# DeltaNet inverse: block transposes on VectorE and a second merge on 64x64 blocks

## Chip, cores, metric

One core of one Trainium2 chip runs the whole kernel. The metric is device microseconds from launch to end; the kernel before was timed in three runs. Engines: TensorE (PE; PEld are its weight loads), VectorE (DVE), ScalarE (ACT), GpSimd (POOL), SyncE (SP, which here issues DMAs).

## The reference

A trunk of two layers over 1024 tokens of 1024 features, all in float32. The first layer mixes tokens with a gated DeltaNet (8 heads of 128), the second with latent attention; a SwiGLU follows each, and adaLN modulates each. Only the DeltaNet is touched. Per head and chunk of tokens it computes

```python
L = where(strict, einsum(kb, k) * decay, 0)     # strictly lower triangular
u = triangular_solve(L + I, v * beta)           # the kernel forms (I + L)^-1 itself
w = triangular_solve(L + I, kb * exp(g_cum))
attn = einsum(q, k) * decay
# then chunk by chunk, with a carried state S:
#   y = u - w S;  o = q_dec S + attn y;  S = S * exp(g_last) + k_dec^T y
```

and after it a norm, a gate and an output projection. The kernel uses chunks of 128 tokens, so each head has 8 matrices L of 128x128.

## The kernel before

The DeltaNet works head by head. For head h the steps are: K (project keys and queries, `gdn_proj`: 24 products of 128x512 for each half of the tokens at line 202, then a convolution on DVE at line 334), A (`gdn_prep_a`: L of each chunk), V (values and gate), B (`gdn_prep_b`: the transposed inverse U and the masked attention `at`), R (`gdn_rec`: the recurrence over 8 chunks). They are written in the order B of head h+1, R of head h, then K, A, V of head h+2. A planner with a cost model then sets the order of instructions on each engine: it takes what is ready by its model, in order of priority, so projections of a later head fill PE between the small products of B and R. On the chip each engine then runs its own list in that fixed order, and semaphores hold an instruction until its operands are there.

`gdn_prep_b` inverts I + L in two stages. First the four 32x32 diagonal blocks of all 8 matrices at once on DVE: ACT copies them out (line 412), a DVE transpose spreads them over partitions (414), 31 steps of two DVE instructions solve (421, 423), and another DVE transpose brings them back as Xn (425). Then, for four matrices at a time ("half"), two merges:

- A zeroed tile Xs (memset on POOL, 438) gets the inverse diagonal blocks by four ACT copies (441). Xs is block diagonal.
- Merge s = 32: PE transposes Xs (446), ACT copies the result into U (448). U is to hold the transposed inverse. PE multiplies L by the odd blocks of U (459, into `pw`), ACT copies it (461, `w`), PE multiplies by Xs (464, `pv`), and DVE writes the negated blocks into U (466).
- Merge s = 64: the same with 64x64 blocks: PE transposes the whole of U (446), ACT copies it into a second Xs (451), PE multiplies L by the right half of U (459), ACT copies w (461), PE multiplies by Xs (464), DVE writes one 64x64 block (466). All these products contract over 128 partitions and have weights of 128 columns, although only one 64x64 block of the result is used.

In float32 each product is two PE instructions, each with its own weight load; a transpose is one. The SBUF pool `gw` has one buffer for each name unless stated, so both Xs share one slot and each `w` waits for the one before it to be read. The PSUM pool `pe` has two banks, named "e". Tiles called junk take the elementwise output of instructions of which only the row sums are used (lines 379, 400, 520).

Of the kernel before, what the change touches and what calls it, by code (L numbers as in the profile page):

```python
# [9 lines left out]
F32 = mybir.dt.float32  # L10
# [9 lines left out]
P = 128  # L20
# [12 lines left out]
class Trunk:  # L33
# [10 lines left out]
    # ---------------------------------------------------------------- constants  # L44
# [64 lines left out]
    # ---------------------------------------------------------------- adaLN  # L109
    def ada_steps(self, l, m, pool, acc):  # L110
        """acc += the rows of ada_w, each times its c; a step to a row tile"""
# [17 lines left out]
    def ada_ahead(self, l, ms, ps, acc, tag):  # L129
        """the parts ms of layer l, a row tile at a time"""  # L130
        for m in ms:
            yield from self.ada_steps(l, m, self.wraw, acc)
            (self.ada_row if m in (2, 5) else self.ada_cols)(l, m, ps, None, tag, acc)
            yield
            yield
            yield
# [12 lines left out]
    def ada_row(self, l, m, ps, pool, tag="ada_p", acc=None):  # L149
        """mod part m of layer l as a row in DRAM"""  # L150
# [23 lines left out]
    # ---------------------------------------------------------------- weights  # L174
# [5 lines left out]
    def load_w(self, src, shape=(KT, P), bufs=None, pool=None, mul=None, tag="w"):  # L180
        """a weight block of up to [P, 1024] as its two float32r parts"""
# [13 lines left out]
    def mm3(self, out, lts, rts):  # L195
        """sum over pairs of ((lhsT hi, lo), (rhs hi, lo)) of their product, less lo*lo"""
        nc = self.nc
        seq = []
        for (lh, ll), (rh, rl) in zip(lts, rts):
            seq += [(lh, rh), (lh, rl), (ll, rh)]  # L200
        for i, (l, r) in enumerate(seq):
            nc.tensor.matmul(out, l, r, start=(i == 0), stop=(i == len(seq) - 1))  # L202

    # ---------------------------------------------------------------- norm
    def rstd_of(self, x, pool, n=D, junk=None):
        """(mean(x^2)+eps)^-0.5 over the row of x [P, n]"""
# [10 lines left out]
    def rpow(self, out, in_):  # L217
        """in_ ** -0.5"""
        self.nc.gpsimd.tensor_tensor(out=out, in0=in_, in1=self.mh[:, 0:in_.shape[1]], op=ALU.pow)  # L219

    # ---------------------------------------------------------------- gated DeltaNet
    def gdn_gates(self, hi, lo, pool, ps):
        """per-token scalars, token-major, column h*8+chunk: beta, g in parts, exp of the sums of g"""
# [77 lines left out]
    def gdn_proj(self, h, names, hi, lo, res, first=None):  # L301
        """conv and silu of q, k, v and silu of z for head h, feature-major"""
        nc = self.nc
        for nm in names:
# [6 lines left out]
            for s in range(2):  # L311
                # the first two by halves of the features: the first half is there before the other
# [23 lines left out]
                # the taps are halved: silu(2 u) = u (1 + tanh u)  # L336
# [7 lines left out]
    def gdn_decay(self, h, qd, flip, tag):  # L344
        """exp of the sum of g over (j, i], for tokens i >= j of 4 chunks; row i, or row j if flip"""
# [17 lines left out]
    def gdn_prep_a(self, h, kq):  # L363
        """L of each chunk, row i by column j, and the per-token scalars that go with it"""
# [6 lines left out]
        for qd in range(2):  # L371
# [5 lines left out]
            for i in range(4):  # L377
                junk = self.gw.tile([P, P], BF16, name="junk", bufs=2)
# [19 lines left out]
            for i in range(4):  # L398
                junk = self.gw.tile([P, P], BF16, name="junk2", bufs=2)
# [3 lines left out]
    def gdn_prep_b(self, h, kq, pr):  # L403
        """at: the masked attention by source token; U: the transpose of (I + L)^-1"""
# [3 lines left out]
        # 32x32 diagonal blocks, one matrix (and one of 4 column groups) to a partition  # L408
# [26 lines left out]
        for m0 in range(0, M, 4):  # L435
            mh = slice(m0, m0 + 4)
            Xs = self.gw.tile([P, 4, P], F32, name="Xs")
            nc.gpsimd.memset(Xs, 0.0)
# [4 lines left out]
            for s in (32, 64):  # L443
                px = self.pe.tile([P, 4, P], F32, name="e")
                for i in range(4):
                    nc.tensor.transpose(px[:, i], Xs[:, i] if s == 32 else U[:, m0 + i], self.ident)
                if s == 32:
                    nc.scalar.copy(U[:, mh], px)
                else:
                    Xs = self.gw.tile([P, 4, P], F32, name="Xs")  # L450
                    nc.scalar.copy(Xs, px)
                pw = self.pe.tile([P, 4, 64], F32, name="e")
                for i in range(4):
                    m = m0 + i
                    if s == 32:
                        rhs = U[:, m].rearrange("p (a b c) -> p a b c", b=2, c=32)[:, :, 1]
                    else:
                        rhs = U[:, m, 64:128]
                    nc.tensor.matmul(pw[:, i], L[:, m], rhs, start=True, stop=True)  # L459
                w = self.gw.tile([P, 4, 64], F32, name="w")  # L460
                nc.scalar.copy(w, pw)
                pv = self.pe.tile([P, 4, 64], F32, name="e")
                for i in range(4):
                    nc.tensor.matmul(pv[:, i], Xs[:, i], w[:, i], start=True, stop=True)  # L464
                for b in range(0, 4, 2) if s == 32 else (0,):
                    v.tensor_scalar(out=U[b * 32:b * 32 + s, mh, b * 32 + s:b * 32 + 2 * s],
                                    in0=pv[b * 32:b * 32 + s, :, b * 16:b * 16 + s], scalar1=-1.0, op0=ALU.mult,
                                    scalar2=None)
        pr.update(at=at, U=U)

    def gdn_rec(self, h, kq, pr):
# [4 lines left out]
        for half in range(2):  # L476
            on = self.gw.tile([P, 4, P], F32, name="on")
            ss = self.gs.tile([P, 4], F32, name="ss")
            for cc in range(4):
# [39 lines left out]
                junk = self.gw.tile([P, P], BF16, name="junk3", bufs=2)  # L519
                nc.scalar.activation(out=junk, in_=on[:, cc], func=AF.Square, accum_out=ss[:, cc:cc + 1])  # L520
            # rms norm of o with the scale of q folded in
# [17 lines left out]
    def gdn_prologue(self, hi, lo):  # L539
        """the first norm: x goes feature-major while the modulation is worked out, one half of the features first"""  # L540
# [6 lines left out]
        with ExitStack() as st:  # L547
# [10 lines left out]
            def ada(half):  # L558
                """the parts 0 and 1 of the modulation, for half of the features"""
# [52 lines left out]
            # x0[(b, r, m), i, c] = (i == 8 r + c)  # L612
# [9 lines left out]
    def gdn(self, right, outer):  # L622
# [5 lines left out]
        with ExitStack() as s2:  # L628
# [21 lines left out]
            self.gs = s2.enter_context(tc.tile_pool(name="gs", bufs=2))  # L650
            kqv, pr = [{} for _ in range(H)], {}
# [46 lines left out]
    # ---------------------------------------------------------------- output projection  # L698
    def out_w(self, heads, w_out, gate, own=None):
        """rows of w_out for these heads, times the gate"""  # L700
# [3 lines left out]
    def out_row(self, t, h0, ws, x_src, x, raw, oh, ol, bank):  # L704
        """x = a row of x_src + gate * (o @ w_out) over the heads from h0 on"""
# [11 lines left out]
    def out_rows(self, h0, ws, x_src, op, bank, done, raw_t):  # L717
        """row tile by row tile; done(t, row) takes each"""
# [7 lines left out]
    def out_pools(self, l, right):  # L726
        """for the weights of two heads and for rows; they stay open in right"""
# [3 lines left out]
    def gdn_out(self, w_out, x_src, right, bank, before):  # L731
        """the first four heads, to x_dram; the weights of the others stay"""
# [14 lines left out]
    # ---------------------------------------------------------------- SwiGLU  # L747
    # gate and up (rows 1 and 2) of one block of ff, times the halves of d, times the halves of the tokens:
    # one step of Strassen's product in Winograd's form,
    #   S1 = A21 + A22, S2 = S1 - A11, S3 = A11 - A21, S4 = A12 - S2  # L750
    #   T1 = B12 - B11, T2 = B22 - T1, T3 = B22 - B12, T4 = T2 - B21
    #   P1 = A11 B11, P2 = A12 B21, P3 = S4 B22, P4 = A22 T4, P5 = S1 T1, P6 = S2 T2, P7 = S3 T3
    #   U2 = P1 + P6, U3 = U2 + P7
    #   C11 = P1 + P2, C12 = U2 + P5 + P3, C21 = U3 - P4, C22 = U3 + P5
# [9 lines left out]
    def ffn_pair(self, t, xs, pool, ps):  # L764
        """token tiles 2 t and 2 t + 1 (rows xs) into the right-hand operands; B1, B2 are the even and the odd tiles"""
# [736 lines left out]
```

## Time and profile before

| | us |
|---|---|
| median of 3 runs | 2642.77 (2641.49 to 2646.53) |
| span of the profiled execution, first to last instruction | 2633.9 |
| PE busy | 2519.0 (96%) |
| DVE busy | 1957.7 (74%) |
| ACT busy | 1182.6 (45%) |
| POOL busy | 182.6 (7%) |

The profiled execution's time from launch to end is not given apart from its span. The page says for each engine how long it was busy, and follows a chain back from the last instruction through whatever released each step. A busy share over the whole span mixes stages: the DeltaNet runs from about 100 to 740 us, and stretches and waits of it are asked for separately. An instruction's duration on PE includes its way through the array, so products that follow each other closely have starts nearer together than their durations.

### The profile page before, as it was taken

Reading aid. Unit: us, or ns where it says so; the run is one execution under the profiler, and the core shown is the slowest. Engines: PE = TensorE matmul, PEld = TensorE weight load, DVE = VectorE, ACT = ScalarE, POOL = GpSimd, SP = SyncE. Lnnn points to the kernel's source line nnn. Section 1 sums busy time; section 2 is a strip of 40 time slices with the busy share of each in tenths; the row PEclk is TensorE's granted clock in tenths of the full one; section 3 lists DMA queues with packets and bytes.
Section 4 is the critical chain, followed back from the end, with each engine's and each line's share of the span. In section 5 each row is a group of like instructions: output and inputs, shape, how many; then the busy total and the mean of one; then the engine's idle time right before and its main releaser. Section 6 shows DMA issues by size and latency. Waiting matters only on the chain.

```text
span 2633.9 us, 35735 instructions
## 1 busy us (share of the span) xinstructions
PE 2519.0 (96%) x12821; PEld 2074.6 (79%) x12821; DVE 1957.7 (74%) x3732; ACT 1182.6 (45%) x2390; POOL 182.6 (7%) x337
## 2 busy tenths in 40 slices
PE   5999899999899999999999899999999999999998
PEld 4777777777778888888888798888779888887786
DVE  5886788888758887877586766667568777774778
ACT  5555455555556222323334575555374233232433
POOL 1211112221000000000000010000010000000000
PEclk8999999999999999999999999999999999999999
DMA  6111222321544544545854521112653332335634
GB/s 227 41 33 33 73 73 85 93 89 49 168 160 158 168 151 152 176 130 176 281 173 147 160 74 59 47 51 77 202 175 97 105 104 92 108 104 211 237 96 144
DMA packets 258705, 327.62 MB, mean 124 GB/s; under 512 B 17578, under 2 KB 176448, under 8 KB 258528
## 3 DMA queue, kind: packets, MB, share of 16 engines
q1 hardware_dynamic: 235840, 284.37, 34.4%
q10 hardware_dynamic: 22688, 40.97, 4.1%
q8 instruction: 101, 1.65, 0.3%
q14 instruction: 76, 0.62, 0.1%
HBM read 247.16 MB, written 78.14 MB: 124 GB/s over the span
## 4 chain that ended last, share of the span: by engine, by line
PE 77%; DVE 11%; ACT 4%; DMA 3%; POOL 2%; issue 2%; SPq 0%; POOLq 0%; DVEq 0%; ACTq 0%
PE pd L965 14%; PE nrm_p L202 14%; PE pj L202 13%; PE pd L202 10%; PE P L202 7%; PE pd L1282 3%; PE po L202 2%; DVE cacc L334 2%; PE pq L202 1%; PE tp L1325 1%; PE e L464 1%; PE e L459 1%; DVE X L423 1%; ACT Xs L441 1%; DVE st L421 1%
## 5 line engine op out<-in xcount | busy, mean ns | idle before, releaser
L965 PE MATMUL pd<-wlo,gh 128*128 128x512 f32 x616 | 243.4, 396 | 2.3 <-DVE wlo L178 1.9
L965 PE MATMUL pd<-whi,gl 128*128 128x512 f32 x616 | 241.4, 394 | 1.3 <-DVE gl L178 1.2
L965 PE MATMUL pd<-whi,gh 128*128 128x512 f32 x616 | 236.7, 394 | 5.0 <-ACT gh L177 4.6
L202 PE MATMUL pj<-hThi,whi 128*128 128x512 f32 x480 | 196.5, 409 | 0.0
L202 PE MATMUL pj<-hThi,wlo 128*128 128x512 f32 x480 | 196.0, 408 | 0.0
L202 PE MATMUL pj<-hTlo,whi 128*128 128x512 f32 x480 | 194.8, 406 | 0.0
L177 ACT CAST gh<-wraw 128x1024 fp32r<-128x1024 f32 x84 | 82.3, 979 | 247.5 <-PE pd L965 208.8
L177 ACT CAST whi<-wraw 128x1024 fp32r<-128x1024 f32 (+3 forms) x105 | 100.6, 960 | 136.8 <-DMA wraw<-in_ffn_w_gate_dram 50.2
L219 POOL TENSOR_TENSOR nrm_r<-nrm_r,mh 128x1 f32<-128x1 f32 x56 | 37.7, 674 | 1594.1 <-DVE nrm_r L213 1585.1
L965 PEld LDWEIGHTS pd<-wlo,gh 128*128 128x128 f32 x616 | 116.2, 189 | 33.5 <-DVE wlo L178 8.3
L178 DVE TENSOR_TENSOR gl<-wraw,gh 128x1024 fp32r<-128x1024 f32 x84 | 95.3, 1134 | 62.2 <-ACT gh L177 62.0
L965 PEld LDWEIGHTS pd<-whi,gh 128*128 128x128 f32 x616 | 116.0, 188 | 32.1 <-ACT gh L177 5.9
L178 DVE TENSOR_TENSOR wlo<-wraw,whi 128x1024 fp32r<-128x1024 f32 (+3 forms) x105 | 117.2, 1116 | 28.2 <-ACT whi L177 26.9
L965 PEld LDWEIGHTS pd<-whi,gl 128*128 128x128 f32 x616 | 116.2, 189 | 27.4 <-DVE gl L178 2.2
L202 PE MATMUL nrm_p<-T,xrow 128*128 128x512 f32 (+1 forms) x576 | 133.7, 386 | 0.0
L202 PE MATMUL nrm_p<-T,ow_hi 128*128 128x512 f32 (+1 forms) x600 | 132.0, 368 | 0.0
L202 PE MATMUL nrm_p<-T,ow_lo 128*128 128x512 f32 (+1 forms) x552 | 125.8, 376 | 0.0
L202 PEld LDWEIGHTS nrm_p<-T,xrow 128*128 128x128 f32 x576 | 105.1, 188 | 23.7
L202 PEld LDWEIGHTS nrm_p<-T,ow_hi 128*128 128x128 f32 x600 | 103.6, 188 | 20.8 <-ACT fh L785 0.2
L202 PEld LDWEIGHTS nrm_p<-T,ow_lo 128*128 128x128 f32 x552 | 97.8, 188 | 20.6
L334 DVE SCALAR_TENSOR_TENSOR cacc<-cr,cwc,cacc 128x512 f32<-128x512 f32 x144 | 108.7, 761 | 6.0 <-ACT cacc L332 5.5
L202 PEld LDWEIGHTS pj<-hThi,wlo 128*128 128x128 f32 x480 | 91.5, 191 | 15.4
(527 smaller groups left out, 6459.9 us busy)
## 6 DMA issues: line engine op xcount, KB each, us to landing
wraw<-in_ada_w_dram SPq DMA_DIRECT2D x80, 512.0 KB, 4.2
wraw<-in_ffn_w_gate_dram SPq DMA_DIRECT2D x44, 512.0 KB, 4.1
wraw<-in_ffn_w_up_dram SPq DMA_DIRECT2D x44, 512.0 KB, 4.6
gd_S<-sx ACTq DMA_DIRECT2D x88, 256.0 KB, 2.6
B<-in_ffn_w_down_dram SPq DMA_DIRECT2D x40, 512.0 KB, 6.6
wraw<-gd_S SPq DMA_DIRECT2D x40, 512.0 KB, 4.5
gd_A<-co ACTq DMA_DIRECT2D x66, 256.0 KB, 2.7
wraw<-in_gdn_w_in_dram SPq DMA_DIRECT2D x32, 512.0 KB, 4.1
```

Source lines behind the costliest of these rows:

```text
L177: nc.scalar.copy(hi, raw)
L178: nc.vector.tensor_tensor(out=lo, in0=raw, in1=hi.bitcast(F32), op=ALU.subtract)
L202: nc.tensor.matmul(out, l, r, start=(i == 0), stop=(i == len(seq) - 1))
L219: self.nc.gpsimd.tensor_tensor(out=out, in0=in_, in1=self.mh[:, 0:in_.shape[1]], op=ALU.pow)
L334: nc.vector.scalar_tensor_tensor(out=acc, in0=cr[:, j:j + 512], scalar=self.cw[:, j, ch:ch + 1], in1=acc, op0=ALU.mult, op1=ALU.add)
L421: v.tensor_tensor(out=t[:, 0:n], in0=Lr[:, j, j + 1:32].rearrange("p (i o) -> p i o", o=1).broadcast_to([P, n, 8]), in1=X[:, j:j + 1].broa ...
L423: v.tensor_tensor(out=X[:, j + 1:32], in0=X[:, j + 1:32], in1=t[:, 0:n], op=ALU.subtract)
L441: nc.scalar.copy(Xs[pb, :, b * 32:b * 32 + 32].rearrange("p m (r c) -> p m r c", c=8), Xn[pb, :, :, mh].rearrange("p c r m -> p m r c"))
L459: nc.tensor.matmul(pw[:, i], L[:, m], rhs, start=True, stop=True)
L464: nc.tensor.matmul(pv[:, i], Xs[:, i], w[:, i], start=True, stop=True)
L965: nc.tensor.matmul(acc[t], x[:, j, ts], y[:, j], start=(j0 + j == 0 and k == 0), stop=(j0 + j == NJ - 1 and k == 2))
L1282: nc.tensor.matmul(sc[:, 0:nm], q[:, ts], k[:, cs], start=(i == 0), stop=(i == 4 and not last))
```

## The change

In `gdn_prep_b` Xs becomes one tile for all heads, zeroed once before the loop; the ACT copies overwrite its diagonal blocks each time. A DVE transpose of 32x32 blocks writes U from Xs directly, in place of four PE transposes and the ACT copy. The first merge is otherwise as before. The second merge takes the lower left 64x64 block of L (partitions 64 to 127) as weights and the lower right block of U; it transposes only the upper left 64x64 block of U on PE, and both copies and the last product are 64 partitions wide. Three junk tiles go from two buffers to one, two of them under one name. Comments are taken out.

```diff
@@ gdn_prep_a and gdn_rec
-                junk = self.gw.tile([P, P], BF16, name="junk", bufs=2)
+                junk = self.gw.tile([P, P], BF16, name="junk")
-                junk = self.gw.tile([P, P], BF16, name="junk2", bufs=2)
+                junk = self.gw.tile([P, P], BF16, name="junk2")
-                junk = self.gw.tile([P, P], BF16, name="junk3", bufs=2)
+                junk = self.gw.tile([P, P], BF16, name="junk2")
@@ gdn_prep_b
-            Xs = self.gw.tile([P, 4, P], F32, name="Xs")
-            nc.gpsimd.memset(Xs, 0.0)
+            Xs = self.xs
...
-            for s in (32, 64):
-                px = self.pe.tile([P, 4, P], F32, name="e")
-                for i in range(4):
-                    nc.tensor.transpose(px[:, i], Xs[:, i] if s == 32 else U[:, m0 + i], self.ident)
-                if s == 32:
-                    nc.scalar.copy(U[:, mh], px)
-                else:
-                    Xs = self.gw.tile([P, 4, P], F32, name="Xs")
-                    nc.scalar.copy(Xs, px)
...
+            v.transpose(out=U[:, mh], in_=Xs)
+            pw = self.pe.tile([P, 4, 64], F32, name="e")
+            for i in range(4):
+                rhs = U[:, m0 + i].rearrange("p (a b c) -> p a b c", b=2, c=32)[:, :, 1]
+                nc.tensor.matmul(pw[:, i], L[:, m0 + i], rhs, start=True, stop=True)
+            w = self.gw.tile([P, 4, 64], F32, name="w")
+            nc.scalar.copy(w, pw)
+            pv = self.pe.tile([P, 4, 64], F32, name="e")
+            for i in range(4):
+                nc.tensor.matmul(pv[:, i], Xs[:, i], w[:, i], start=True, stop=True)
+            for b in (0, 2):
+                pb = slice(b * 32, b * 32 + 32)
+                v.tensor_scalar(out=U[pb, mh, b * 32 + 32:b * 32 + 64], in0=pv[pb, :, b * 16:b * 16 + 32],
+                                scalar1=-1.0, op0=ALU.mult, scalar2=None)
+
+            lo, up = slice(0, 64), slice(64, 128)
+            px = self.pe.tile([64, 4, 64], F32, name="e")
+            pw = self.pe.tile([64, 4, 64], F32, name="e")
+            for i in range(4):
+                nc.tensor.matmul(pw[:, i], L[up, m0 + i, lo], U[up, m0 + i, up], start=True, stop=True)
+            for i in range(4):
+                nc.tensor.transpose(px[:, i], U[lo, m0 + i, lo], self.ident[lo, lo])
+            w = self.gw.tile([P, 4, 64], F32, name="w")
+            nc.scalar.copy(w[lo], pw)
+            x = self.gw.tile([64, 4, 64], F32, name="xw")
+            nc.scalar.copy(x, px)
+            pv = self.pe.tile([64, 4, 64], F32, name="e")
+            for i in range(4):
+                nc.tensor.matmul(pv[:, i], x[:, i], w[lo, i], start=True, stop=True)
+            v.tensor_scalar(out=U[lo, mh, up], in0=pv, scalar1=-1.0, op0=ALU.mult, scalar2=None)
@@ gdn, before the loop over heads
+            self.xs = self.gw.tile([P, 4, P], F32, name="Xs")
+            nc.gpsimd.memset(self.xs, 0.0)
```

## Rows read from the trace of the kernel before

**Rows 1.** The page: busy time of each engine, and the chain by engine.

```profile
PE 2519.0 (96%) x12821; PEld 2074.6 (79%) x12821; DVE 1957.7 (74%) x3732; ACT 1182.6 (45%) x2390; POOL 182.6 (7%) x337
...
PE 77%; DVE 11%; ACT 4%; DMA 3%; POOL 2%; issue 2%; SPq 0%; POOLq 0%; DVEq 0%; ACTq 0%
```

**Rows 2.** Windows, the DeltaNet alone: busy us (x instructions) by engine, clock, DMA, GB/s.

```profile
100.00:740.00 640.00, 596.76 (x3348) 484.86 (x3347) 515.45 (x1369) 333.92 (x880) 123.59 (x167) 0.99 0.25 75
```

**Rows 3.** Windows of 25 us in the DeltaNet.

```profile
200.00:225.00 25.00, 22.73 (x155) 19.09 (x154) 12.37 (x32) 14.70 (x40) 2.19 (x4) 1.00 0.11 32
...
250.00:275.00 25.00, 21.86 (x101) 18.07 (x100) 22.24 (x49) 9.57 (x21) 4.17 (x6) 0.86 0.15 43
...
575.00:600.00 25.00, 22.18 (x111) 17.13 (x110) 23.68 (x46) 12.53 (x27) 6.42 (x7) 1.00 0.38 106
```

**Rows 4.** Waits, 100 to 740 us: who waited for whom, total us, times, longest.

```profile
PE c L433 <- DVE at L434: 12.2, 6, 3.1
...
PE e L446 <- ACT Xs L441: 11.7, 15, 2.1
...
PEld e L459 <- ACT U L448: 3.1, 13, 0.4
```

**Rows 5.** The chain that ended last, 100 to 740 us, by line.

```profile
by line: PE pj L202 19.4%; DVE cacc L334 6.2%; issue 4.9%; PE e L464 4.5%; PE e L459 4.5%; DVE X L423 4.2%; ACT Xs L441 3.9%; DVE st L421 3.7%; PE e L446 2.6%; POOL co L219 2.3%; POOL rk L219 2.2%; PE d L507 2.2%; DVE wlo L178 2.1%; PE d L5
```

**Rows 6.** The chain in order of time, 203 to 218 us: start, us, what.

```profile
207.52 0.63 PE e L446 x4
...
213.05 0.44 PE e L446 x4
213.49 0.84 PE e L459 x8
...
216.07 0.53 POOL Xs L438
```

**Rows 7.** Lines with shapes kept apart, 0 to 900 us: busy us, mean ns, idle before.

```profile
L178 DVE TENSOR_TENSOR wlo<-wraw,whi 128x1024 fp32r<-128x1024 f32 x41 | 50.9, 1241 | 11.3 <-ACT whi L177 11.3
...
L464 PE MATMUL e<-w,Xs 128*128 128x64 f32 x256 | 33.4, 273 | 0.1
L459 PE MATMUL e<-U,L 128*128 128x64 f32 x256 | 33.1, 272 | 0.1
...
L459 PEld LDWEIGHTS e<-U,L 128*128 128x128 f32 x256 | 31.1, 191 | 3.3 <-ACT U L448 3.1
...
L441 ACT COPY Xs<-Xn 32x128 f32<-32x128 f32 x64 | 27.0, 422 | 8.9 <-POOL Xs L438 5.4 <-DVE Xn L425 2.8
...
L461 ACT COPY w<-e 128x256 f32<-128x256 f32 x32 | 11.9, 372 | 12.9 <-PE e L459 12.9
...
L446 PE MATMUL e<-ident,Xs 128*128 128x128 f32 x64 | 10.2, 283 | 12.5 <-ACT Xs L441 11.7 <-POOL co L219 0.9
...
L414 DVE STREAM_TRANSPOSE Lr<-Ld 128x1024 f32<-128x1024 f32 x8 | 9.9, 1240 | 1.8 <-ACT Ld L412 1.7
...
L448 ACT COPY U<-e 128x512 f32<-128x512 f32 x16 | 9.4, 585 | 2.9 <-PE e L446 2.8
...
L438 POOL MEMSET Xs<- 128x512 f32 x16 | 8.4, 526 | 83.5 <-PE e L464 83.5
...
L425 DVE STREAM_TRANSPOSE Xn<-X 128x256 f32<-128x256 f32 x8 | 5.3, 668 | 0.1
```

**Rows 8.** Timeline of PE at two places: start, us, what.

```profile
81.41 0.40 PE L202 MATMUL pj<-hTlo,whi 128*128 128x512 f32 x1
81.64 0.40 PE L236 MATMUL c<-hThi,at 128*32 128x512 f32 x1
...
505.05 1.84 PE L143 MATMUL e<-ones,wraw 128*128 128x1 f32 x16
506.75 0.47 PE L355 MATMUL c<-R,m_gt 128*128 128x512 f32 x1
```

**Rows 9.** Lines of the weight loads, whole span, shapes kept apart.

```profile
L236 PEld LDWEIGHTS c<-hThi,at 128*32 128x32 f32 x16 | 1.7, 108 | 2.1 <-ACT cr L330 0.3
```

More of the change, by code (lines that the diff above doesn't have):

```diff
@@ L442, in gdn_prep_b @@
                                Xn[pb, :, :, mh].rearrange("p c r m -> p m r c"))
-            for s in (32, 64):
-                px = self.pe.tile([P, 4, P], F32, name="e")
-                for i in range(4):
-                    nc.tensor.transpose(px[:, i], Xs[:, i] if s == 32 else U[:, m0 + i], self.ident)
-                if s == 32:
-                    nc.scalar.copy(U[:, mh], px)
-                else:
-                    Xs = self.gw.tile([P, 4, P], F32, name="Xs")
-                    nc.scalar.copy(Xs, px)
[L452 to L468, printed above, removed]
```

## The prediction

> **What bounds the kernel now.** The page's first part has TensorE (PE) busy 96% of the span, and its chain of waits is PE for 77% [rows 1]. The change touches only the DeltaNet, so the next view is that stretch by itself, 100 to 740 us: PE is busy 596.8 of 640 us (93%), DVE 515.5 (81%), ACT 333.9, POOL 123.6, at a granted clock of 0.99 [rows 2]. So PE is idle 43 us there. In 25-us steps the picture alternates: with the merges of a head (200 to 225 us) DVE is busy 12.4 us and PE 22.7; where the next head's triangular solve runs (575 to 600) it is DVE 23.7 and PE 22.2 [rows 3]. The reader should see two engines taking turns, with the code of the change in the turn that belongs to PE.
>
> The waits say what PE's 43 idle us are [rows 4]: 11.7 us in 15 waits (0.78 us each) are the first transposes of a merge waiting for ACT's copies into Xs, and the weight loads of the first product wait 3.1 us for ACT's copy into U. Another 12.2 us are at L433, which the change leaves alone. The chain of the stretch has the merges on it: L464 4.5%, L459 4.5%, the Xs copies 3.9%, L446 2.6% [rows 5], and around 205 to 217 us it goes through one half of four matrices step by step [rows 6].
>
> **Counts.** Eight heads, two halves each: 16 halves. Each has 4 transposes ahead of each merge (64 instructions at L446 from Xs, as many from U) and 4 products by L and 4 by the transposed block in each merge, two instructions apiece (256 at L459, 256 at L464) [rows 7].
>
> **Part 1, the first transposes leave PE.** Four of them take 0.44 us on the chain [rows 6], 0.11 each; 64 x 0.11 = 7.0 us of PE work. This I count in full.
>
> **Part 2, the second merge on 64x64 blocks.** It stays at 128 product instructions at L459's place and 128 at L464's, and 64 transposes, 320 in all. Moving columns of the products stay at 64; weights shrink from 128 to 64 columns, the transposes' moving columns too. Eight products take 0.84 us on the chain [rows 6], 0.105 each. What sets this pace? The 16 products at L143 have one moving column and full weights, and the next product starts 1.70 us after their first: 0.106 each [rows 8]. So one moving column or 64, the pace is the weight load's. Loads of 128 columns take 191 ns [rows 7], of 32 columns 108 ns [rows 9]: 0.86 ns a column, so 64 columns should take 55 ns less. No row has 64-column weights in a dense stream, so the saving lies between 0 and 0.055 us an instruction, 0 to 17.6 us together. I take 0.04, nearer to the load rows, because the 64 moving columns and the issue of two instructions must fit in what is left: 320 x 0.04 = 12.8 us.
>
> **Part 3, the DVE transpose.** Block transposes take 668 ns for 256 elements a partition and 1240 for 1024 [rows 7]; in between, 512 elements take 668 + 572/3 = 859 ns. That is 16 x 0.86 = 13.7 us more on DVE. From Xs to U it was a PE transpose and a copy: 0.63 + 0.585 us [rows 6, 7]; now it is 0.86, if DVE is free. Hidden by: DVE's idle half in the merge stretch [rows 3]. If that cover is missing, the transpose queues behind what DVE has; its longest frequent instruction is the 1.24-us split of a weight block [rows 7]. The new wait also works backward: while DVE stands at the transpose until ACT's fourth copy is done, everything queued behind it stands too: the next head's solve, the convolutions that feed Q and K, the r and S updates of the recurrence, and PE then waits for those. PE today stands 0.78 us for the same copies, so DVE may stand about as long. Bounds for PE's waiting: all of 11.7 + 3.1 = 14.8 us gone (copies and transposes fully covered), or 16 x 1.24 = 19.8 us more. I take 0.3 us more for each half, 4.8 us, nearer to zero than to the upper bound since the path from Xs to U itself gets 0.35 us shorter.
>
> **Part 4, Xs, ACT and POOL.** The memset (526 ns, 16 times) goes; the memset at 216.07 us in the chain shows what hung on it: Xs was one slot for both merges, so the second half's memset and four copies (4 x 0.42 us) began only after the first half's last product [rows 6, 7]. Now they wait only for the first merge's products and the DVE transpose. That lets the second half start earlier; its worth is inside the 14.8 us bound above and I count nothing of it. ACT loses a 585-ns copy into U, and its other copy of that shape shrinks to about 372 ns (the 128x256 copy of w) [rows 7], 16 x 0.80 = 12.8 us; ACT is busy 52% here, so nothing. The accumulation junk tiles go from two buffers to one, each written by one engine alone in its own order: nothing, and if a release did bind, at most one 0.3-us pass of ACT or DVE per use. The single memset ahead of the loop sits in POOL's idle time.
>
> **Sum.** -7.0 - 12.8 + 4.8 = -15.0 us on a span of 2633.9, so 2618.9. The median of the three timed runs, 2642.8, lies 8.9 us above that span; what lies around the span is not touched, so the forecast is 2642.8 - 15.0 = 2627.8, say **2628 us** (0.57% faster). Behind the merges DVE is late next: its busy share of the stretch rises from 81% to 529/625, 85%, still under PE's.
>
> A rule of the Trainium skill speaks against part 2. The rows first: where PE goes from full weights to 32-column ones (81.41 to 81.64 us) starts are 0.23 us apart, though each product lasts 0.40 [rows 8]: no drain is seen for narrower columns. No row shows weights that also start on the upper half of the partitions. The Trainium skill, TensorEngine Tiling (Array Packing), section Key Properties, says that a change of tiling mode, not just of tile, drains TensorE. By that rule every pass from projection products to 64x64 ones and back would pay.
>
> **Rivals.**
> 1. *Drains at each change of shape.* Per half the small products come in two groups (product with transposes; last product), so four changes, 64 in all; a drain is at most the 0.40 - 0.23 = 0.17 us by which a product outlasts the next start [rows 8]: 64 x 0.17 = 10.9 us, 2628 + 11 = 2639. For: projections do fill in between. Against: the row without a drain. Chance 0.12.
> 2. *Narrow weights buy nothing* (the pace of 0.105 is issue, not load), or DVE's share rules the turn: only part 1 counts, -7.0 + 4.8 = -2.2, up to -7.0 if no wait is added: 2636 to 2641. For: the same 0.105 at 1 and 64 columns fits an issue limit as well. Against: load time follows columns [rows 7, 9]. Chance 0.16.
> 3. *The transpose waits in DVE's queue and PE behind it* (the slower one). Place: the first product of each half. It decides where the added wait passes 19.8/16 = 1.24 us a half. At that point all gain is gone; if DVE also stands 0.78 us for ACT and both reach PE, 0.86 + 0.78 + about 0.5 behind a split = 2.1 us a half, 34 us against 19.8: +14, 2657. Longer waits also drop the clock: 250 to 275 us, with a 3.1-us wait at L433 in it, was granted 0.86, 25 x 0.14 = 3.5 us lost [rows 3, 4]. For: in-order DVE, 81% busy, and the order of all queues is planned anew. Against: DVE is half idle beside the merges. Chance 0.16.
> 4. *More than forecast:* loads in full proportion (17.6), transposes 7.0, and half of the 14.8 us of waits gone because the halves now overlap: -32, 2611. Chance 0.08.
>
> **How the numbers follow.** The forecast has 0.48 and alone reaches from 2618 to 2638. About 0.2% (5.3 us) can be told from no change. Faster: nearly all of the forecast (0.46), rival 4 (0.08), under half of rival 2 (0.07): 0.61. Same: rival 1 (0.11), the rest of rival 2 (0.09), the forecast's edge (0.02): 0.22. Slower: rival 3 and a stray: 0.17. Leaving out rival 3's upper part and rival 4's lower, the range is 2611 to 2648.
>
> **What would show it.** Part 1: L446's rows with Xs gone and 16 stream transposes of about 0.86 us. Part 2: second-merge loads near 136 ns, and eight of its products in about 0.5 us instead of 0.84; 0.84 again means rival 2, and a projection product after them starting late means rival 1. Part 3: PE's wait at the first product, now on DVE, near 1 us a half; 2 us or more and low clocks mean rival 3. PE busy in the stage about 20 us less; if it is less by that and the stage isn't, DVE has become the bound, and that would make the forecast wrong.

## The result, and the profile after

The changed kernel took 2613.32 us (median) against 2642.57 us for the kernel before: ratio 0.99, 95% interval [0.9878, 0.9922], 29 us less. Repeated later it took 2621.97 us against 2641.76: ratio 0.9936 [0.9915, 0.9957], 17 us less by the ratio and 20 by the medians. The forecast was 15 less, so the direction was right and the size somewhat too small.

Executions of one kernel differ by some 9 us with the clock that TensorE is granted, and the three that count of the first measurement (a fourth took 3079 us at a mean clock of 0.747) were all of the faster kind while those of before were not, so the repeat is the better measure of the gain.

Windows of the first 100 us, of before, of the first measurement and of the repeat (columns as in [rows 2]):

```profile
0.00:100.00 100.00, 73.24 (x351) 57.51 (x352) 64.86 (x137) 57.19 (x81) 10.62 (x55) 0.90 0.52 165
```

```profile
0.00:100.00 100.00, 75.00 (x359) 59.00 (x360) 65.58 (x138) 58.90 (x84) 10.62 (x55) 0.90 0.52 165
```

```profile
0.00:100.00 100.00, 73.60 (x326) 58.19 (x327) 59.15 (x119) 54.78 (x77) 10.28 (x53) 0.81 0.52 165
```

The granted clock there is 0.90, 0.90 and 0.81, and the first ACT copy into Xs comes at 167.9, 166.2 and 175.3 us. The partner of before, with a span of 2633.9 us, is therefore the first measurement, whose span is 2611.6: 22.3 us less. All rows of "after" below are from that execution. The page, answering to [rows 1], and the windows that answer to [rows 2] and to the first two of [rows 3]:

```profile
PE 2505.5 (96%) x12757; PEld 2058.1 (79%) x12757; DVE 1962.5 (75%) x3748; ACT 1173.5 (45%) x2374; POOL 171.5 (7%) x322
...
PE 77%; DVE 11%; ACT 4%; DMA 3%; issue 2%; POOL 2%; ACTq 0%; POOLq 0%; DVEq 0%; SPq 0%
```

```profile
100.00:740.00 640.00, 602.48 (x3366) 480.36 (x3365) 528.49 (x1405) 332.44 (x886) 114.28 (x153) 0.98 0.26 79
...
200.00:225.00 25.00, 23.59 (x161) 18.59 (x159) 17.65 (x50) 16.04 (x45) 1.38 (x5) 1.00 0.11 32
...
250.00:275.00 25.00, 21.69 (x108) 17.60 (x107) 21.71 (x60) 10.06 (x28) 4.21 (x6) 0.86 0.13 40
```

Over the whole span PE's busy time fell by 13.5 us and its idle time from 114.9 to 106.1. The windows do not hold the same work before and after. From 100 to 740 us PE is busy for longer than before (596.8 us): it idles less, and work from behind the recurrence, which now ends at 739.0 us and not at 753.7, has moved in; the table below goes by a window that ends with the recurrence. From 200 to 225 us DVE is busy 17.7 us and not 12.4, because the merges begin there at 211.4 us and not at 205.6, and the end of the solve lies ahead of them. Over the merges alone, all heads, DVE's busy share rose from 62% to 69%, and PE's stayed at 93%. Lines with shapes kept apart, answering to [rows 7] (busy us, mean ns, idle before):

```profile
L447 PE MATMUL e<-U,L 128*128 128x64 f32 x128 | 17.6, 281 | 4.2 <-DVE U L443 3.4 <-DVE t L529 0.8
...
L443 DVE STREAM_TRANSPOSE U<-Xs 128x512 f32<-128x512 f32 x16 | 11.4, 711 | 11.6 <-ACT Xs L441 11.6
L462 PE MATMUL e<-U,L 64*64 64x64 f32 x128 | 11.2, 230 | 0.0
...
L462 PEld LDWEIGHTS e<-U,L 64*64 64x64 f32 x128 | 9.0, 139 | 5.0 <-issue 2.8 <-PE d L497 0.4 <-PE c L355 0.4
...
L464 PEld LDWEIGHTS e<-ident,U 64*64 64x64 f32 x64 | 4.0, 108 | 1.1
```

L447 and L452 are now the first merge's products; L462, L464 and L471 are the second merge's, its transposes and its last products. The 64-column loads take 139 ns (191 before), the DVE transpose 711 ns (forecast 859). The waits that answer to [rows 4], and DVE's at its transpose (total us, times, longest):

```profile
PE c L433 <- DVE at L434: 12.8, 5, 4.7
PE e L447 <- DVE U L443: 3.4, 3, 2.2
PE e L471 <- ACT xw L468: 1.9, 4, 0.6
PE e L447 <- DVE t L529: 0.8, 1, 0.8
...
DVE U L443 <- ACT Xs L441: 11.6, 16, 1.7
```

Where PE stood 11.7 us in 15 waits for the Xs copies, it now stands 4.2 us in 4; DVE stands in its place, 0.73 us a half (0.78 forecast). One half of a head in the chain of waits, answering to [rows 6] (start, us, what):

```profile
214.34 0.84 PE e L447 x8
...
217.42 0.47 PE pj L202 x2
217.89 0.60 PE e L462 x8
218.49 0.34 PE e L464 x4
218.84 0.89 PE pj L202 x3
219.73 0.67 PE e L471 x8
```

Eight narrow products take 0.60 us where 0.84 were, and four transposes 0.34 where 0.44 were. The three projection products after them take 0.89 us, where two take 0.47 ahead of them: the way out of the narrow shape and back into it costs something.

### The profile page after: what moved, and what is told of

The parts are those of the page before. It is cut to its first block, busy times and chain, and to the rows that moved or that the text cites. A ratio compares the mean times of both kernels' runs of the same rounds, so it can differ in the third digit from the quotient of the medians.

```text
span 2611.6 us, 35555 instructions
## 1 busy us (share of the span) xinstructions
PE 2505.5 (96%) x12757; PEld 2058.1 (79%) x12757; DVE 1962.5 (75%) x3748; ACT 1173.5 (45%) x2374; POOL 171.5 (7%) x322
## 4 chain that ended last, share of the span: by engine, by line
PE 77%; DVE 11%; ACT 4%; DMA 3%; issue 2%; POOL 2%; ACTq 0%; POOLq 0%; DVEq 0%; SPq 0%
PE pd L971 14%; PE nrm_p L202 14%; PE pj L202 14%; PE pd L202 10%; PE P L202 8%; PE pd L1288 3%; PE po L202 2%; DVE cacc L334 2%; PE pq L202 1%; PE tp L1331 1%; DVE X L423 1%; DVE st L421 1%; ACT Xs L441 1%; DVE wlo L178 1%; PE d L511 1%
## 5 line engine op out<-in xcount | busy, mean ns | idle before, releaser
L219 POOL TENSOR_TENSOR nrm_r<-nrm_r,mh 128x1 f32<-128x1 f32 x56 | 37.4, 669 | 1585.3 <-DVE nrm_r L213 965.7
L202 PEld LDWEIGHTS nrm_p<-T,ow_lo 128*128 128x128 f32 x552 | 98.0, 189 | 20.4
L202 PEld LDWEIGHTS pj<-hTlo,whi 128*128 128x128 f32 x480 | 92.0, 192 | 15.4
```

## The experiments

Three parts of the change can be had alone: **D**, the DVE transpose for the first merge; **N**, the narrow second merge; **S**, Xs kept for the first merge alone and zeroed once, with the second merge's block in another slot. All eight combinations were run, each on a chip where the kernel before ran too (medians 2641.3 to 2641.8). The kernels with one part were made from the kernel before, those with two from the changed one, so these have the junk tiles of the change as well. In us, 0.001 of ratio is 2.64.

**D alone.**
```diff
-   px = self.pe.tile([P, 4, P], F32, name="e")      # first merge only
-   ... four PE transposes of Xs, ACT copy into U
+   v.transpose(out=U[:, mh], in_=Xs)
```


> Only the DVE block transpose in place of the four PE transposes and the ACT copy of the first merge; Xs keeps its one slot and its memset, the second merge stays wide. Theory (PE's work in the merge turn sets the time): 7.0 us of PE work and part of the 14.8 us of PE waits go, 7 to 12 us faster than before, 2631 to 2636. Rival (the freed slot of Xs and the overlap of the halves made the gain): at most the 7.0 us, 2636 or more. Rival (DVE is in the way): no gain, 2640 to 2650.

2635.05 us, ratio 0.9975 [0.9958, 0.9991]: -6.6 us. PE's waits in the DeltaNet:

```profile
PE c L433 <- DVE at L434: 14.9, 6, 4.9
PE e L459 <- DVE U L445: 4.5, 5, 1.9
```

The waits for the path from Xs to the first product fell from 11.7 to 4.5 us, and those at L433 rose from 12.2 to 14.9: PE's idle time as a whole stayed (table below). What is left of the gain is PE's work.

**N alone.** The second merge as in the changed kernel, its transposed block in the slot of Xs, PE transposes for the first merge.

> Only the second merge on 64x64 blocks; the first keeps its PE transposes and copy, and the narrow transposed block goes into the slot of Xs, so the order of the halves is as before. Theory: 320 instructions at 58 instead of 112 ns is 17.3 us less, five changes of shape a half at 0.09 us is 7.2 us more: about 10 us faster, 2630 to 2635, with PE's waits on Xs still near 12 us. Rival (narrow blocks buy nothing in the end): 2640 to 2645.

2638.58 us, ratio 0.9997 [0.9981, 1.0013]: nothing that the times show (the table's last column takes the clock out). The wait at the copies is what it was:

```profile
PE e L445 <- ACT Xs L441: 12.0, 15, 2.1
```

**The junk tiles alone.**
```diff
-   junk = self.gw.tile([P, P], BF16, name="junk", bufs=2)
+   junk = self.gw.tile([P, P], BF16, name="junk")
    ... likewise junk2, and junk3 as junk2
```


> Only the junk tiles from two buffers to one. Theory: nothing waits for them, within 3 us of before, and it shows how much a new plan of the order moves by itself. Rival (the planner's new order is a large part of the 29 us): a shift of 8 us or more either way.

2643.78 us, ratio 1.0012 [0.9995, 1.0029]: no change can be told from the times, as the prediction's part 4 had it; with the clock taken out, as in the last column of the table below, they are 4.2 us slower.

**D and N without S.** The changed kernel with Xs and the second merge's block in one slot again.
```diff
-   Xs = self.xs
+   Xs = self.gw.tile([P, 4, P], F32, name="Xs")
+   nc.gpsimd.memset(Xs, 0.0)
...
-   x = self.gw.tile([64, 4, 64], F32, name="xw")
+   x = self.gw.tile([P, 4, P], F32, name="Xs")[0:64, :, 0:64]
...                                                  # and no Xs ahead of the loop
```


> The changed kernel, but Xs is zeroed anew for each half and shares its slot with the second merge's transposed block, as before the change. Theory (work on PE): gives back under 5 us, 2613 to 2618. Rival (overlap of the halves through the freed slot): gives back 8 us or more, 2621 to 2626, and PE waits on the Xs copies return.

2629.31 us, ratio 0.9961 [0.9943, 0.9979]: 6.6 us of the repeat's gain is gone, give or take 7, between the theory's price and the rival's. Waits, where the memset for the next half waits for the last product (L472) of the half before:

```profile
POOL Xs L439 <- PE e L472: 40.0, 9, 12.5
...
PE e L448 <- DVE U L444: 5.7, 6, 2.2
```

**The changed kernel again.**

> The changed kernel once more, so that it is timed beside the others on one chip. If its three equal times of 2613.3 were all of its better start (executions of one kernel differ by some 9 us with the granted clock in the first 100 us), the median is 2613 to 2622 and the gain over before 20 to 25 us. Otherwise 29 us again.

2621.97 us, ratio 0.9936 [0.9915, 0.9957]; its rows at L447 and L462 are those of the first measurement.

**S alone.**
```diff
-   Xs = self.gw.tile([P, 4, P], F32, name="Xs")
-   nc.gpsimd.memset(Xs, 0.0)
+   Xs = self.xs                                     # zeroed once, ahead of the loop
...
-   Xs = self.gw.tile([P, 4, P], F32, name="Xs")     # second merge
+   Xs = self.gw.tile([P, 32, 32], F32, name="Lr")[:, 0:16].rearrange("p (m a) b -> p m (a b)", m=4)
```


> The kernel before with one change: Xs is one tile zeroed once, and the transposed block of the second merge (still 128 wide, from PE and ACT) goes into the slot of Lr, so the second half's copies into Xs need not wait for the second merge of the first half. Theory (the slot is the largest part): the second half starts about 6 us after the first instead of 10.5, and 10 to 16 us are gained, 2626 to 2632. Rival (the slot is only worth something once the merges are shorter on PE): under 5 us, 2637 or more.

2643.31 us, ratio 1.0006 [0.9988, 1.0023]: nothing, although the halves do overlap (table). PE still waits for ACT's copies:

```profile
PE e L445 <- ACT Xs L440: 8.0, 8, 2.4
```

**The DVE transpose twice** in the changed kernel.
```diff
    v.transpose(out=U[:, mh], in_=Xs)
+   v.transpose(out=U[:, mh], in_=Xs)
```


> The changed kernel with each DVE block transpose done twice, 16 x 0.71 = 11.4 us more on DVE in the merge stretch and 0.71 us more before the first product of each half. Theory (PE sets the time there and fills the wait with projections): under 4 us slower than the changed kernel. Rival (DVE and its order set the time now): 8 us or more slower.

2616.61 us, ratio 0.992 [0.9899, 0.9942]: 11.3 us more of DVE work cost nothing that can be told.

```profile
L443 DVE STREAM_TRANSPOSE U<-Xs 128x512 f32<-128x512 f32 x16 | 11.4, 711 | 9.9 <-ACT Xs L441 9.8
L444 DVE STREAM_TRANSPOSE U<-Xs 128x512 f32<-128x512 f32 x16 | 11.3, 703 | 0.0
```

**Narrow weights on all 128 partitions.** The second merge of the changed kernel contracts 128 rows again, with 64 weight columns; it tells whether the pauses around the narrow products come with the halved rows or with the halved columns.
```diff
-   nc.tensor.matmul(pw[:, i], L[up, m0 + i, lo], U[up, m0 + i, up], start=True, stop=True)
+   nc.tensor.matmul(pw[:, i], L[:, m0 + i, lo], U[:, m0 + i, up], start=True, stop=True)
...
-   nc.tensor.transpose(px[:, i], U[lo, m0 + i, lo], self.ident[lo, lo])
+   nc.tensor.transpose(px[:, i], U[:, m0 + i, lo], self.ident)
...
-   nc.tensor.matmul(pv[:, i], x[:, i], w[lo, i], start=True, stop=True)
+   nc.tensor.matmul(pv[:, i], x[:, i], w[:, i], start=True, stop=True)   # x in a tile zeroed once
```


> The changed kernel with a second merge that contracts over all 128 partitions (the added rows are zero) and has 64-column weights; its transposes have 128 moving columns again. Theory (the 0.09 us at each change of shape comes with the halved rows, since 32-column weights over 128 rows showed none): product starts stay near 58 ns apart, the pauses before and after the groups go, 16 x 4 x 0.09 = 5.8 us less against 64 x 0.054 = 3.5 us more for the transposes: 0 to 4 us faster than the changed kernel. Rival (it comes with the narrow columns): pauses stay, 2 to 5 us slower than the changed kernel.

2623.12 us, ratio 0.9941 [0.992, 0.9962], as the changed kernel. PE's timeline of the changed kernel, then of this one (start, us, what):

```profile
217.49 0.40 PE L202 MATMUL pj<-hTlo,whi 128*128 128x512 f32 x1
217.82 0.68 PE L462 MATMUL e<-U,L 64*64 64x64 f32 x8
218.42 0.41 PE L464 MATMUL e<-ident,U 64*64 64x64 f32 x4
218.77 0.50 PE L202 MATMUL pj<-hThi,wlo 128*128 128x512 f32 x1
219.10 0.39 PE L202 MATMUL pj<-hThi,whi 128*128 128x512 f32 x1
219.33 0.40 PE L202 MATMUL pj<-hTlo,whi 128*128 128x512 f32 x1
```

```profile
218.36 0.39 PE L202 MATMUL pj<-hTlo,whi 128*128 128x512 f32 x1
218.68 0.68 PE L462 MATMUL e<-U,L 128*64 128x64 f32 x8
219.29 0.63 PE L464 MATMUL e<-ident,U 128*64 128x128 f32 x4
```

From a projection product to the next one 0.23 us pass (219.10 to 219.33); to the first narrow product 0.33 (217.49 to 217.82), and 0.32 with all 128 rows (218.36 to 218.68). Into a wide product of the merges it is 0.235 in the kernel before, so the pause comes with the change to 64 columns, not with the rows. One pause does go with all 128 rows: from the four transposes to a projection product 28 ns pass, where 64 rows have 146. These transposes have 128 moving columns again, and their starts are 109 ns apart, as those of the wide ones, although their weights have 64 columns. By the starts of all such pairs in the traces (medians): narrow products follow one another at 58 ns where the wide ones did at 112, narrow transposes at 56 (109); but 328 ns lie between a projection product and L462 (231 between two projection products), 149 between L462 and L464, 146 between L464 and a projection product (28 from the wide transposes), 320 or more from a projection product to L471 (most have a wait in them) and 148 from L471 to L447: about 0.09 us more at each of five passages a half. The passage from L462 to L464 is not a change of shape, both being 64x64; what makes that pause is open.

**D and S with the wide second merge.** The changed kernel, with the second merge 128 wide as before and its block in the slot of Lr.

> The changed kernel, but its second merge is 128 wide again (the transposed block in the slot of Lr): the DVE transpose and the free slot of Xs without the narrow blocks. Theory (PE's work adds up, its idle time falls with the free slot and the shorter path together): PE work from the first Xs copy to the end of the recurrence 5 to 8 us above the changed kernel at full clock, PE idle in it below 38 us, 5 to 9 us slower than the changed kernel, 2626 to 2631. Rival (the three parts are worth something only all together): back to 2635 or more.

2624.81 us, ratio 0.9939 [0.9919, 0.9959]: not to be told from the changed kernel.

```profile
PE c L433 <- DVE at L434: 11.6, 5, 3.8
PE e L447 <- DVE U L443: 3.6, 3, 2.3
```

**N and S without D.** The changed kernel, with four PE transposes of Xs and an ACT copy into U in place of the DVE transpose.

> The changed kernel, but U of the first merge comes from PE transposes and an ACT copy again: the narrow blocks and the free slot of Xs without the DVE transpose. Theory: PE work 6 to 9 us more at full clock, idle below 40 us, 6 to 12 us slower than the changed kernel, 2627 to 2634. Rival (only all together): 2635 or more.

2627.42 us, ratio 0.9963 [0.9945, 0.9981]; PE waits for the copies again, though less often than before:

```profile
PE e L445 <- ACT Xs L441: 6.8, 8, 2.3
```

**The other large wait.** In the changed kernel, ACT copies the attention scores out of PSUM and DVE multiplies them in SBUF, the two quarters' decays in two slots, so that L433 need not wait for DVE.
```diff
-   dec = self.gdn_decay(h, qd, True, "decT")
+   dec = self.gdn_decay(h, qd, True, ("decT", "dec")[qd])
...
-   v.tensor_tensor(out=at[:, qd * 4:qd * 4 + 4], in0=pa, in1=dec, op=ALU.mult)
+   ms = slice(qd * 4, qd * 4 + 4)
+   nc.scalar.copy(at[:, ms], pa)
+   v.tensor_tensor(out=at[:, ms], in0=at[:, ms], in1=dec, op=ALU.mult)
```


> The changed kernel with one edit elsewhere in the same function: ACT copies the attention scores out of PSUM, DVE multiplies them by the decay in SBUF, and the second quarter's decay takes the slot of the other decay tile. Theory (what is left of PE's idle time is led by L433 waiting behind the solve in DVE's queue, 12.8 us, and the clock falls behind such waits): these waits and some of the half-clock stretches go, 6 to 14 us faster than the changed kernel, 2607 to 2616. Rival (the wait only moves, to the recurrence or to ACT's queue): within 4 us of the changed kernel.

2622.7 us, ratio 0.9927 [0.9908, 0.9947], as the changed kernel. The wait at L433 is gone and its like stands at the recurrence:

```profile
PE d L490 <- DVE S L515: 12.1, 6, 3.7
```

So that wait is not the buffer's alone: in this one try PE stood as long at the next place where it needs something from DVE. No version tried is faster than the changed kernel by more than its interval.

**The eight combinations together.** The start of the second half after the first, and the sum of a head's merges (first ACT copy into Xs to the last write of U) over eight heads, are read from the traces; PE's idle time is from the window that starts with the first such copy and ends with PE's last instruction of the recurrence. The last column is an estimate with the clock taken out: the span of each execution on record times its mean granted clock, averaged, less the same for the kernel before.

| kernel | second half starts after, us | merges, us | PE idle, us | ratio | against before, us | the same, clock taken out |
|---|---|---|---|---|---|---|
| before | 10.3 to 11.5 | 171.1 | 40.4 | 1 | 0 | 0 |
| S | 5.9 to 6.6 | 152.0 | 37.4 | 1.0006 | +1.6 | -1.6 |
| D | 9.9 to 13.1 | 168.0 | 40.3 | 0.9975 | -6.6 | -9.6 |
| N | 9.9 to 15.3 | 168.6 | 40.2 | 0.9997 | -0.8 | -5.3 |
| D, N | 9.4 to 13.9 | 164.5 | 41.0 | 0.9961 | -10.3 | -14.7 |
| N, S | 6.0 to 7.5 | 144.0 | 35.8 | 0.9963 | -9.8 | -9.9 |
| D, S | 5.3 to 6.8 | 139.1 | 32.0 | 0.9939 | -16.1 | -15.7 |
| D, N, S (repeat) | 5.3 to 7.3 | 135.6 | 34.2 | 0.9936 | -16.9 | -20.4 |

For each part four pairs of rows differ in it and in no other part. D is worth -6.6, -17.7, -9.5 and -7.1 us, mean -10; S +1.6, -9.5, -9.0 and -6.6, mean -6; N -0.8, -3.7, -11.4 and -0.8, mean -4. Each ratio has about 0.0018 on either side, so one difference has 7 us and a mean of four about 3.5 (squares added): D is shown, S is too but by little, N only just. That S gives nothing alone and 6.6 to 9.5 us beside D or N is what the rows say; a single one of these differences does not prove it.

The last column is sharper: executions of one kernel differ by 2 us in it (standard deviation), where their times differ by 4 to 6, so each entry has 1 to 2 us on either side. By it D is worth 10.9 us in the mean, N 5.9 and S 4.5, and S again gives little alone (1.6). N alone is worth 5.3 us, but its executions had a mean clock of 0.9830 where those of before had 0.9846, which is 4 us. The junk tiles alone cost 4.2 us by it, through their buffers or through the new order of the plan, which no run tells apart. Only the kernels with two or three parts have them, so two of the four pairs of each part come out short by as much, and each mean by some 2 us.

The windows behind the table, for before, then D with S, then the changed kernel, then N alone:

```profile
167.90:753.70 585.80, 545.45 (x3111) 443.26 (x3112) 462.60 (x1205) 305.73 (x822) 108.27 (x142) 0.99 0.26 80
```

```profile
173.70:747.50 573.80, 541.81 (x3047) 440.11 (x3047) 471.31 (x1223) 302.74 (x807) 97.09 (x127) 0.98 0.26 81
```

```profile
166.20:739.00 572.80, 537.68 (x3056) 428.66 (x3055) 469.08 (x1222) 298.09 (x807) 97.29 (x127) 0.98 0.27 84
```

```profile
167.90:755.70 587.80, 547.59 (x3110) 437.18 (x3111) 460.97 (x1205) 302.98 (x822) 100.51 (x142) 0.97 0.26 80
```

Busy time holds the stretches at 1.2 GHz, in which the eight products at L433 take 2.08 us (from 262.87 us in the changed kernel) where they take 1.05 at 2.4 (from 255.40). By the clock records of these windows there are 13.7 us of it in before, 20.5 with D and S, 23.9 in the changed kernel and 34.1 with N alone (13.7 in the changed kernel's repeat). Counted at half, PE's work at full clock is 545.5 - 6.9 = 538.6, 541.8 - 10.3 = 531.5, 537.7 - 12.0 = 525.7 and 547.6 - 17.1 = 530.5. So N alone takes 8.1 us of work off PE, and its profiled execution gave that back in clock: 34.1 us at 1.2 GHz against 13.7.

## Why the prediction was right in direction and too small

**Part 1, the transposes leave PE: right.** Forecast -7.0 us. D alone is -6.6 in time; its PE work is 529.8 by the same count, -8.8.

**Part 2, the narrow second merge: the mechanism right, the term mis-sized.** Forecast -12.8 from 0.04 us an instruction. The pace fell by 54 ns an instruction, about the 52 by which the products' load is shorter (191 to 139), so the load did set the pace of the wide products (rival 2, that narrow weights buy nothing, is refuted at its cause): 320 x 0.054 = 17.3 us. For the 64 transposes among the 320 the narrower weights were not what counted: with 64 weight columns and 128 moving ones (the run on all 128 partitions) they keep the wide pace, 109 ns. But five passages a half take back 5 x 16 x 0.09 = 7.2, which leaves 10.1; PE's work says 8.1 (N alone) and 5.8 (531.5 - 525.7, with D and S there; 3.8 by the repeat). Measured in time it is 4 us, give or take 3.5, and 5.9 with the clock taken out.

**Rival 1, drains at each change of shape: such pauses are real, at about half its price for each.** It had 64 changes of at most 0.17 us; there are 80 of 0.09. That the engine drains in them is not shown. The step that misled was the row at 81.41 us [rows 8], where going to 32-column weights showed 0.23, no pause; it was taken to hold for 64 columns. The Trainium skill, TensorEngine Tiling (Array Packing), section Key Properties, says that a change of tiling mode drains TensorE. The pause into 64 columns agrees, with 128 rows or with 64, 128x64 being a mode of its own on that page; the row with 32 columns does not show one, and the pause between L462 and L464, both 64x64, has no change of mode to come from.

**Part 3, the DVE transpose: wrong, the wait that it added did not come.** The forecast had PE wait 4.8 us more at the first product. It waits less: 14.8 us at the copies and at U became 4.2 at L447 and 1.9 at L471. By D alone PE's idle time as a whole stays (40.3 us against 40.4); it falls only with S (32.0 to 35.1 with D and S). The step that failed is "I take 0.3 us more for each half": it charged the transpose's 0.86 us behind the copies, while in the trace PE has projection products and the other half to run until U is there (4 waits in 16 halves). DVE has room for it twice over (transposes doubled: 0.992), so rival 3, PE waiting behind DVE's queue, is refuted. DVE does stand 0.73 us a half, as forecast, and the time shows nothing that is late by it.

**Part 4, Xs with a tile of its own: counted at nothing, and worth about 6 us, with 3.5 on either side.** The prediction saw the chain (memset and copies of the second half after the first half's last product, [rows 6]) and put its worth inside the waits' bound without a value. Freed, the second half starts 5 to 7 us after the first and not 10 to 12, and a head's merges are 2.4 us shorter by S alone (171.1 - 152.0 over eight) and 3.6 beside D and N (164.5 - 135.6). By itself that changes nothing in the time (S alone, +1.6); its trace still has PE standing 8.0 us for the copies. Taken back from the changed kernel it costs 6.6. With the clock taken out the mean is 4.5. The junk tiles, counted at nothing, are not told from nothing by the times; with the clock taken out they cost 4.2 us.

**The sum.** In the window of the table the first measurement has PE's work at -12.9 (forecast -19.8), PE's idle time at 35.1 - 40.4 = -5.3 (forecast +4.8) and +5.1 for 10.2 us more at 1.2 GHz (not forecast): -13.0 or so; the repeat, with the clock of before, has 568.8 - 585.8 = -17.0. So in this window the gain is about the forecast's, and that is partly luck: two errors of opposite sign, less work taken off PE and less waiting than forecast, nearly cancel. What the whole kernel gains beyond it lies behind the recurrence (below). Rival 4's mechanism, halves that overlap, is real, without its full price because the pauses take their part; it had 0.08 and should have had more, for its cause stood in the chain of before. The 8.9 us that the prediction read between span and time come mostly from setting one execution's span against the median of others: the profiled execution of the changed kernel took 2613.28 us with a span of 2611.6. The forecast, a difference, does not hang on it.

**Left open.** Work behind the recurrence, which the change does not touch, is 7.6 us shorter in the first measurement (2611.6 - 739.0 against 2633.9 - 753.7) and 4.4 in the repeat. In the table's six other kernels it lies between 0.7 us longer and 5.3 shorter. By the clock records 25.6 us of it were at 1.2 GHz in before and 18.7 in the first measurement, which makes 3.5 of the 7.6; no run tells whether that is the change's doing or chance.

## What to carry to other kernels

A slot shared by two steps that look independent can hold back a whole second half: look in the chain for a memset or a copy that follows the other step's last product, and give it a price, together with whatever shortens the path that it releases. Narrowing small TensorE products pays where the weight load sets their pace (54 ns an instruction for 64 columns less here), but each passage to and from other shapes took about 0.09 us. Groups of eight products and four transposes kept about half of their saving; longer groups should keep more, which no run tried. A wait for an engine that is late can move to the next place that needs the same engine (L433). And times that scatter with the granted clock can be compared more sharply as span times clock.

## What the runs showed of the hardware that was not expected

- A DVE block transpose of 512 elements a partition takes 711 ns, though 256 take 668 and 1024 take 1240 [rows 7]: a straight line between the two gave 859, 21% too much.
- The rows of a weight load hardly count: 64 columns took 139 ns on 64 partitions and 142 on 128 (load rows at L462 in the changed kernel and in the one with all rows). The columns are not all that does: the loads of transposes took 108 ns for 64 columns (L464) and 140 for 128 (L446 before). The Trainium skill, TensorE: Matmul & The Clock Gate, section LDWEIGHTS (loading the stationary operand), says the same of rows; its formula, columns over 1.2, would give 53 ns for 64 columns and 107 for 128, where the load rows of products show 139 and 191, but the step between them, 52, agrees with it, and the products' starts, 58 and 112 ns apart, lie near it.
- One wait cost nearly as much again in clock. After PE had waited 3.3 us at L433 (259 to 263 us in the changed kernel, 0.69 us busy of 4), the next 4 us, all busy, were granted 0.50, that is 1.2 GHz, and the following 0.83, so 4 x (0.50 + 0.17) = 2.7 us of a busy engine were lost:

```profile
259.00:263.00 4.00, 0.69 (x5) 0.50 (x5) 3.93 (x9) 0.15 (x1) 0.68 (x1) 0.82 0.13 26
263.00:267.00 4.00, 4.00 (x17) 3.81 (x18) 3.16 (x11) 1.75 (x6) 0.63 (x1) 0.50 0.29 105
267.00:271.00 4.00, 4.00 (x22) 3.33 (x21) 2.43 (x10) 1.28 (x6) 0.00 (x0) 0.83 0.00 0
```
